# Two more raw weight buffers in the MLP, with a place of its own for block B22, in a tile that otherwise holds a branch's output

## The chip, the core and the metric

The kernel runs on one core of a Trainium2 chip. PE is the matrix engine (PEld its weight loads), DVE the vector engine, ACT the scalar engine, POOL and SP issue transfers here (POOL also does a few small operations). The metric is device time in microseconds (us) of one execution; runs without a profile give the median, and one execution with a profile gives the trace that is read below.

## The reference, cut to what matters

The program is two layers of an encoder trunk on 256 tokens of width 2048, all in float32. Each layer has a token-mixing half (one wide projection, three branches A, B and C, gates, an output projection) and an MLP half. The change lies in the MLP half:

```
D_MODEL, SEQ, DEPTH = 2048, 256, 2
D_FF = 4 * D_MODEL
for l in range(DEPTH):
    ...                                  # branches A, B, C, gates, merge
    x = x + merged @ w_out[l]
    h2 = rms_norm(x, norm2_g[l])
    u = jax.nn.relu(h2 @ w_up[l])        # (256, 2048) @ (2048, 8192)
    x = x + (u * u) @ w_down[l]          # (256, 8192) @ (8192, 2048)
return rms_norm(x, final_g)
```

## The kernel before, in words

**Weights.** 256 tokens make every product one pass over its weights, which come from HBM in pieces of 256 rows by 512 columns (512 KB, called a raw piece). Each piece is split into two parts that PE takes at its fast float32 rate: `whi`, a rounded copy made by ACT (L189, L207), and `wlo`, the rest, made by DVE (L190, L210). A product is three matmuls of 128x128 by 128x512 (L225, L226, L227): high by high, high by low, low by high.

**Slots.** The work is one list, `slots`, in the order in which PE runs it (`run_steps`). A plain slot is one raw piece: 12 matmuls. `ahead(i)`, called in the middle of slot i, writes the conversion of slot i+3 (`AHEAD = 3`, four pairs of `whi`/`wlo`), then `fetch`, which issues loads of further raw pieces on SP's queue, then `fetch_sums`. There are four raw buffers (`RAW_BUFS = 4`), and `st["free"]` counts how many pieces have been used up. SP issues its loads in the order of the program, and each waits until its buffer has been read, most often until DVE has written the `wlo` that reads it.

**The MLP.** Four times per layer, an up stage (four blocks of 512 columns of `w_up`, L243 and L244) makes a quarter of U = relu(h2 w_up)^2, and a down stage multiplies it by 2048 rows of `w_down`. The down stage goes over two column blocks at once (a pair, `add_pair`). A pair has eight steps s of 256 rows. Five of them are two plain slots each. The three steps in `SEVEN = (1, 3, 4)` take seven block products in place of eight: four slots `a`, `b`, `c`, `d` of 6, 6, 6 and 3 matmuls (`seven`). The 256 by 1024 piece of weights is cut into blocks B11, B12 (upper) and B21, B22 (lower). Slot `a` converts B11 and B21 (one raw piece); slots `b` and `c` convert four sums of blocks, held in a tile T called `tsum`; slot `d` converts B22. In the last quarter only the first pair is done so, and the other two blocks are plain units.

**T.** T has two places, taken in turn. A T is filled by a load on SP's queue (L182: B11 and B12), then by an adding transfer on POOL's queue, which waits for that load to land (L183: adds B12 and B22), and then by two additions on DVE in slot `a` (L208, L209). `fetch_sums` starts the T of the block after next once slot `c` has been written (`st["used"]`). So the T for s = 4 is started at slot `c` of s = 1, in the same pair.

**B22.** Before, B22 comes in a raw buffer of its own, of which it fills half (L168, 256 KB). Slot `a` takes both the buffer of B11/B21 and that of B22, and both count as free only after slot `d`.

**The tile.** The pool `yT` has two buffers, of 12 KB a partition, for the outputs of the branches (`ycT`, `yaT`, `ybT`) in turn. In the MLP one of them holds `SU`, the sums of U's blocks for the seven products; the other holds `ybT`, which is no longer read there.

Of the kernel before, what the change touches and what calls it, by code (L numbers as in the profile page):

```python
# [10 lines left out]
F32 = mybir.dt.float32  # L11
FR = mybir.dt.float32r
# [7 lines left out]
DEPTH = 2  # L20
# [11 lines left out]
BLK = 512  # L32
# [6 lines left out]
RAW_BUFS = 4  # L39
SEVEN = (1, 3, 4)  # L40
# [31 lines left out]
def encoder_trunk(ctx: ExitStack, tc: tile.TileContext, I, out: bass.AP):  # L72
    nc = tc.nc

    def pool(name, bufs=1, space=None):
        kw = {} if space is None else {"space": space}
        return ctx.enter_context(tc.tile_pool(name=name, bufs=bufs, **kw))

    one = pool("one")
    raw_p = pool("raw", RAW_BUFS)  # L80
    hl_p = pool("hl", AHEAD + 1)
    y_p = pool("yT", 2)
# [30 lines left out]
    def start(gen):  # L113
        lanes.append([gen, 0])
# [18 lines left out]


    slots, raws, summed = [], [], []
    st = {"dma": 0, "cv": 0, "free": 0, "sum": 0, "used": 0}
    raw_t, hl_t = {}, {}

    def add_raw(w, r, c, half=False):
        raws.append((w[r:r + 256, c:c + BLK], half))  # L140
        return len(raws) - 1

    def add_unit(w, r0, c0, nkc, act, after, form=None):
        u = {"act": act, "after": after, "n": nkc, "form": form}
        for s in range(nkc // 2):
            slots.append({"u": u, "s": s, "kind": "plain", "raw": add_raw(w, r0 + 256 * s, c0)})

    def add_pair(w, r0, c0, nkc, act, sums, half, middle, after):

        u = {"act": act, "after": after, "n": nkc, "form": "pair", "sums": sums, "half": half, "middle": middle}  # L150
        for s in range(nkc // 2):
            r = [add_raw(w, r0 + 256 * s, c0 + n * BLK, half=s in SEVEN and n == 1) for n in range(2)]
            if s in SEVEN:
                q = {"r": r, "w": w[r0 + 256 * s:r0 + 256 * (s + 1), c0:c0 + 2 * BLK], "i": len(summed)}
                summed.append(q)
                for kind in "abcd":
                    slots.append({"u": u, "s": s, "kind": kind, "q": q})
            else:
                for n in range(2):
                    slots.append({"u": u, "s": s, "kind": "plain", "raw": r[n], "n": n})  # L160

    def fetch(upto):
        while st["dma"] <= min(upto, len(raws) - 1):
            j = st["dma"]
            t = raw_p.tile([128, 2, BLK], F32, tag="raw", name="raw")
            src, half = raws[j]
            if half:
                nc.sync.dma_start(out=t[:, 1, :], in_=src[128:256, :])  # L168
            else:
                nc.sync.dma_start(out=t, in_=src.rearrange("(k p) f -> p k f", p=128))  # L170
            raw_t[j] = t
            st["dma"] += 1

    def fetch_sums():

        while L.get("T") is not None and st["sum"] < min(st["used"] + 2, len(summed)):
            q = summed[st["sum"]]
            if q["i"] >= L["T_end"]:
                return
            T = q["T"] = L["T"][:, q["i"] % 2]  # L180
            w = q["w"]
            nc.sync.dma_start(out=T[:, 1:3, :], in_=w[0:128, :].rearrange("p (n f) -> p n f", n=2))  # L182
            nc.gpsimd.dma_start(out=T[:, 1:3, :], in_=w[:, BLK:2 * BLK].rearrange("(k p) f -> p k f", p=128),  # L183
                                accum_op=ALU.add)
            st["sum"] += 1

    def lead(hi, lo, src):

        nc.scalar.activation(out=hi, in_=src, func=ACTF.Copy)  # L189
        nc.vector.tensor_tensor(out=lo, in0=src, in1=hi.bitcast(F32), op=ALU.subtract)  # L190

    def convert(upto):
        while st["cv"] <= min(upto, len(slots) - 1):
            sl = slots[st["cv"]]
            kind = sl["kind"]
            hi = hl_p.tile([128, 2, BLK], FR, tag="hi", name="whi")
            lo = hl_p.tile([128, 2, BLK], FR, tag="lo", name="wlo")
            if kind == "plain":
                lead(hi, lo, raw_t.pop(sl["raw"]))
                st["free"] += 1  # L200
            else:
                q = sl["q"]
                if kind == "a":
                    q["b0"], q["b1"] = [raw_t.pop(r) for r in q["r"]]
                b0, b1, T = q["b0"], q["b1"], q["T"]
                if kind == "a":
                    nc.scalar.activation(out=hi, in_=b0, func=ACTF.Copy)  # L207
                    nc.vector.tensor_tensor(out=T[:, 0, :], in0=T[:, 2, :], in1=b0[:, 0, :], op=ALU.add)  # L208
                    nc.vector.tensor_tensor(out=T[:, 3, :], in0=T[:, 0, :], in1=b0[:, 1, :], op=ALU.add)  # L209
                    nc.vector.tensor_tensor(out=lo, in0=b0, in1=hi.bitcast(F32), op=ALU.subtract)  # L210
                elif kind == "b":
                    lead(hi, lo, T[:, 0:2, :])
                elif kind == "c":
                    lead(hi, lo, T[:, 2:4, :])
                    st["used"] += 1
                else:
                    lead(hi[:, 1, :], lo[:, 1, :], b1[:, 1, :])
                    st["free"] += 2
            hl_t[st["cv"]] = (hi, lo)
            st["cv"] += 1  # L220

# [73 lines left out]

    def ahead(i):
        convert(min(i + AHEAD, 2 * i + 1))
        fetch(st["free"] - 1 + RAW_BUFS)
        fetch_sums()

    def four_banks(half, name):
# [122 lines left out]
    L = {}  # L424
# [323 lines left out]
    def after_up(n):  # L748
        def f(ps):
            c = L["c"]  # L750
            if n == 0:
                c["U"] = one.tile([128, KD, 2, S], FR, tag="Y", name="U")
                if "T" not in c:
                    c["T"] = True
                    L["T"] = one.tile([128, 2, 4, BLK], F32, tag="merged", name="tsum")
                    L["T_end"] = len(summed) * (c["l"] + 1) // DEPTH
            U = c["U"]
            E = [w2_p.tile([128, 2, S], F32, tag="E", name="u") for _ in range(2)]
            for tl, j0, w in L["groups"]:
                e = E[j0 // 2][:, j0 % 2:j0 % 2 + w, :]  # L760
                nc.scalar.activation(out=e, in_=tl[:, :, S:2 * S], func=ACTF.Copy)
                nc.vector.tensor_tensor(out=e, in0=tl[:, :, 0:S], in1=e, op=ALU.add)
            for e in E:
                nc.vector.scalar_tensor_tensor(out=e, in0=e, scalar=0.0, in1=e, op0=ALU.max, op1=ALU.mult)

            def task():
                for p in range(2):
                    k0 = 4 * n + 2 * p
                    split((U[:, k0:k0 + 2, 0, :], U[:, k0:k0 + 2, 1, :]), E[p])
                    if k0 // 2 in SEVEN:  # L770
                        if k0 // 2 == SEVEN[0]:
                            c["SU"] = y_p.tile([128, len(SEVEN), 2, 4, 128], FR, tag="yT", name="SU")
                        block_sums(c["SU"][:, SEVEN.index(k0 // 2)], E[p])
                    yield
            start(task())
        return f
# [190 lines left out]
    def then(f, g):  # L967
        def both(ps):
            f(ps)

            def later():
                yield
                yield
                yield
                g()
            start(later())
        return both

    for l in range(DEPTH):
        h_in = lambda: L["c"]["norm"].T  # L980
        w_in = I["w_in"][l]
        for unit in range(9):
            f = after_qkv(unit)
# [3 lines left out]
        for br, b, kcs, wname, yname in (("C", 2, 4, "w_proj_c", "ycT"), ("A", 0, 6, "w_proj_a", "yaT"),  # L987
                                         ("B", 1, 6, "w_proj_b", "ybT")):
            for n in range(NB):
                f = after_proj(br, n)  # L990
                if br == "C" and n == NB - 1:
                    f = then(f, queue_attention("B"))
# [15 lines left out]
    with tc.manual_schedule():  # L1008
        vin1 = w2_p.tile([16 * DEPTH, 128], F32, tag="yst", name="vin1")
        nc.sync.dma_start(out=ident, in_=I["c_ident"])  # L1010
        nc.scalar.dma_start(out=vin1, in_=I["norm1_g"].rearrange("l (k p) -> (l k) p", p=128))
        xin = I["x"][0].rearrange("(t p) d -> p t d", p=128)
        for b in range(NB):
            nc.sync.dma_start(out=x[:, :, b * BLK:(b + 1) * BLK], in_=xin[:, :, b * BLK:(b + 1) * BLK])
            fetch(b)
        nc.vector.memset(mhalf, -0.5)
        warm = sm_p.tile([128, 2], F32, tag="ms", name="warm")
        nc.scalar.activation(out=warm, in_=mhalf, func=ACTF.Copy)
        setup_norm1()
        L["c"] = new_layer(0)  # L1020
        norm = L["c"]["norm"]
        pieces = norm.transpose(0)
        next(pieces)
        convert(0)
        next(pieces)
        start(first_norm(norm))
        start(setup_all())
        run_steps()
# [33 lines left out]
```

## Time and profile before

| what | value |
|---|---|
| median of 3 runs without a profile | 2909.21 us (2907.08 to 2910.88) |
| the execution with the profile | 2915.21 us, of which the span is 2913.4 us |
| PE busy | 2862.0 us, 98% of the span |
| DVE, ACT busy | 1794.7 us (62%), 1425.3 us (49%) |
| mean granted clock of PE | 0.994 of full |
| read from HBM | 568.54 MB, 196 GB/s over the span |

A busy share of 98% doesn't say that PE runs at its own pace 98% of the time: the ends of matmuls are modelled, neighbours overlap, and a matmul at a lower clock counts as busy too. The starts of matmuls tell more.

### The profile page before, as it was taken

Reading aid. Unit: us, or ns where it says so; the run is one execution under the profiler, and the core shown is the slowest. Engines: PE = TensorE matmul, PEld = TensorE weight load, DVE = VectorE, ACT = ScalarE, POOL = GpSimd, SP = SyncE. Lnnn points to the kernel's source line nnn. Section 1 sums busy time; section 2 is a strip of 40 time slices with the busy share of each in tenths; the row PEclk is TensorE's granted clock in tenths of the full one; section 3 lists DMA queues with packets and bytes.
Section 4 is the critical chain, followed back from the end, with each engine's and each line's share of the span. In section 5 each row is a group of like instructions: output and inputs, shape, how many; then the busy total and the mean of one; then the engine's idle time right before and its main releaser. Section 6 shows DMA issues by size and latency. Waiting matters only on the chain.

```text
span 2913.4 us, 36216 instructions
## 1 busy us (share of the span) xinstructions
PE 2862.0 (98%) x13816; PEld 2371.6 (81%) x13816; DVE 1794.7 (62%) x2241; ACT 1425.3 (49%) x1818; POOL 155.5 (5%) x146
## 2 busy tenths in 40 slices
PE   9999999999999999999999999999999999999998
PEld 7888888888887878888788888888888878787886
DVE  5465454555677776776644654455556767767675
ACT  5455455444454544545544554454445445444454
POOL 1000001110000000000000000011000000000001
PEclk9999999999999999999999999999999999999999
DMA  7656665555767586675565565655556775856755
GB/s 234 200 151 191 196 175 170 193 183 187 215 205 224 184 243 195 210 219 183 188 214 186 153 197 189 187 161 190 188 187 203 219 229 184 247 179 217 232 180 181
DMA packets 287903, 573.06 MB, mean 197 GB/s; under 512 B 18196, under 2 KB 18382, under 8 KB 287600
## 3 DMA queue, kind: packets, MB, share of 16 engines
q1 hardware_dynamic: 272016, 534.64, 55.8%
q0 software_dynamic: 15376, 35.30, 7.7%
q8 instruction: 108, 1.77, 0.2%
q10 hardware_dynamic: 336, 0.80, 0.1%
q14 instruction: 67, 0.55, 0.1%
HBM read 568.54 MB, written 2.13 MB: 196 GB/s over the span
## 4 chain that ended last, share of the span: by engine, by line
PE 81%; DMA 9%; DVE 6%; issue 2%; ACT 2%; SPq 0%; POOLq 0%; ACTq 0%; DVEq 0%; POOL 0%
PE acc L225 17%; PE acc L226 17%; PE acc L227 17%; PE acc L243 16%; PE acc L244 8%; DMA raw<-in_w_down_dram 5%; DMA tsum<-in_w_down_dram 4%; DVE wlo L190 3%; ACT whi L189 1%; PE ob L553 1%; DVE wlo L210 1%; PE scb L521 0%; DVE tsum L208 0%; DVE x L819 0%; PE xt L400 0%
## 5 line engine op out<-in xcount | busy, mean ns | idle before, releaser
L190 DVE TENSOR_TENSOR wlo<-raw,whi 128x1024 fp32r<-128x1024 f32 (+1 forms) x950 | 1146.2, 1214 | 847.3 <-ACT whi L189 842.7
L189 ACT ACTIVATE whi<-raw 128x1024 fp32r<-128x1024 f32 (+1 forms) x950 | 980.1, 1038 | 928.1 <-PE acc L227 498.2
L243 PE MATMUL acc<-H,whi 128*128 128x512 f32 x2048 | 723.1, 398 | 0.0
L244 PE MATMUL acc<-H,wlo 128*128 128x256 f32 x2048 | 574.6, 281 | 0.0
L225 PE MATMUL acc<-whi,H 128*128 128x512 f32 x1408 | 564.8, 401 | 0.0
L227 PE MATMUL acc<-whi,H 128*128 128x512 f32 x1408 | 550.0, 391 | 0.0
L226 PE MATMUL acc<-wlo,H 128*128 128x512 f32 x1408 | 549.3, 390 | 0.4 <-DVE wlo L190 0.4
L243 PEld LDWEIGHTS acc<-H,whi 128*128 128x128 f32 x2048 | 384.7, 188 | 95.2 <-DVE x L722 0.6
L244 PEld LDWEIGHTS acc<-H,wlo 128*128 128x128 f32 x2048 | 386.7, 189 | 0.4
L225 PE MATMUL acc<-whi,U 128*128 128x512 f32 x772 | 307.0, 398 | 18.9 <-ACT whi L189 15.0
L226 PE MATMUL acc<-wlo,U 128*128 128x512 f32 x772 | 307.2, 398 | 9.6 <-DVE wlo L190 9.3
L225 PEld LDWEIGHTS acc<-whi,H 128*128 128x128 f32 x1408 | 264.9, 188 | 58.8 <-issue 8.1
L227 PEld LDWEIGHTS acc<-whi,H 128*128 128x128 f32 x1408 | 264.6, 188 | 56.8
L226 PEld LDWEIGHTS acc<-wlo,H 128*128 128x128 f32 x1408 | 265.2, 188 | 52.6 <-DVE wlo L190 1.2
L227 PE MATMUL acc<-whi,U 128*128 128x512 f32 x772 | 304.6, 395 | 0.0
L225 PEld LDWEIGHTS acc<-whi,U 128*128 128x128 f32 x772 | 147.2, 191 | 55.5 <-ACT whi L189 20.0
L226 PEld LDWEIGHTS acc<-wlo,U 128*128 128x128 f32 x772 | 147.4, 191 | 45.4 <-DVE wlo L190 15.4
L227 PEld LDWEIGHTS acc<-whi,U 128*128 128x128 f32 x772 | 147.7, 191 | 30.9
L183 POOL DMA_DIRECT2D tsum<-in_w_down_dram x42 | 50.7, 1220 | 1238.5 <-DMA tsum<-in_w_down_dram 1110.1
L189 ACT ACTIVATE whi<-tsum 128x1024 fp32r<-128x1024 f32 x84 | 87.1, 1053 | 33.3 <-DVE tsum L208 19.2
L225 PE MATMUL acc<-whi,M 128*128 128x512 f32 x256 | 101.2, 395 | 0.0
L190 DVE TENSOR_TENSOR wlo<-tsum,whi 128x1024 fp32r<-128x1024 f32 x84 | 99.6, 1219 | 2.1 <-ACT whi L189 2.1
(187 smaller groups left out, 2562.5 us busy)
## 6 DMA issues: line engine op xcount, KB each, us to landing
raw<-in_w_in_dram SPq DMA_DIRECT2D x352, 512.0 KB, 4.2
raw<-in_w_up_dram SPq DMA_DIRECT2D x256, 512.0 KB, 4.3
raw<-in_w_down_dram SPq DMA_DIRECT2D x214, 512.0 KB, 5.3
raw<-in_w_out_dram SPq DMA_DIRECT2D x64, 512.0 KB, 4.1
tsum<-in_w_down_dram SPq DMA_DIRECT2D x42, 512.0 KB, 4.5
tsum<-in_w_down_dram POOLq DMA_DIRECT2D x42, 512.0 KB, 8.0
raw<-in_w_proj_a_dram SPq DMA_DIRECT2D x24, 512.0 KB, 4.6
raw<-in_w_proj_b_dram SPq DMA_DIRECT2D x24, 512.0 KB, 3.5
```

The costliest lines, as they stand in the source:

```text
L183: nc.gpsimd.dma_start(out=T[:, 1:3, :], in_=w[:, BLK:2 * BLK].rearrange("(k p) f -> p k f", p=128), accum_op=ALU.add)
L189: nc.scalar.activation(out=hi, in_=src, func=ACTF.Copy)
L190: nc.vector.tensor_tensor(out=lo, in0=src, in1=hi.bitcast(F32), op=ALU.subtract)
L210: nc.vector.tensor_tensor(out=lo, in0=b0, in1=hi.bitcast(F32), op=ALU.subtract)
L225: nc.tensor.matmul(o, a[0], hi[:, kk, :], start=first, stop=False)
L226: nc.tensor.matmul(o, a[0], lo[:, kk, :], start=False, stop=False)
L227: nc.tensor.matmul(o, a[1], hi[:, kk, :], start=False, stop=last)
L243: nc.tensor.matmul(ps[j], hi[:, kk, fs], a[:, kc, :, :], start=first, stop=False)
L244: nc.tensor.matmul(ps[j][:, S:2 * S], lo[:, kk, fs], a[:, kc, 0, :], start=False, stop=last)
L553: nc.tensor.matmul(o[:, g, :], eT[:, 2 * g + kc, :], c["vb"][:, kc, col:col + 64], start=kc == 0, stop=kc == 1)
```

## The change

The pool `yT` gets a third kind of tile in the MLP, `rawx` (12 KB a partition, `more_room`), in the buffer that held `ybT`. A third of it holds the two B22 blocks of the two T places; the other two thirds are two more raw buffers, used for pieces of `w_up` and of `w_down`'s pairs alone. The counter `st["free"]` becomes a list `free` of free buffers, where None stands for one of the four of the pool `raw`. A buffer goes back to the list as soon as its piece's conversion has been written; that of B11/B21 goes back at slot `a`, not after `d`. B22 is loaded with its T, by `fetch_sums`, and `st["used"]` moves from slot `c` to slot `d`. The `rawx` buffers are dropped from the list when the next piece is not one of the MLP's.

```
-    st = {"dma": 0, "cv": 0, "free": 0, "sum": 0, "used": 0}
+    st = {"dma": 0, "cv": 0, "sum": 0, "used": 0}
+    free = [None] * RAW_BUFS
...
-    def fetch(upto):
-        while st["dma"] <= min(upto, len(raws) - 1):
-            j = st["dma"]
-            t = raw_p.tile([128, 2, BLK], F32, tag="raw", name="raw")
-            src, half = raws[j]
-            if half:
-                nc.sync.dma_start(out=t[:, 1, :], in_=src[128:256, :])
-            else:
-                nc.sync.dma_start(out=t, in_=src.rearrange("(k p) f -> p k f", p=128))
-            raw_t[j] = t
+    def fetch():
+
+        while free and st["dma"] < len(raws):
+            src, mlp = raws[st["dma"]]
+            b = free.pop(0)
+            if b is not None and not mlp:
+                continue
+            t = raw_p.tile([128, 2, BLK], F32, tag="raw", name="raw") if b is None else b
+            nc.sync.dma_start(out=t, in_=src.rearrange("(k p) f -> p k f", p=128))
+            raw_t[st["dma"]] = (t, b)
             st["dma"] += 1
 
+    def take(j):
+        t, b = raw_t.pop(j)
+        return t, lambda: free.append(b)
+
+    def more_room(c):
+
+        T = one.tile([128, 2, 4, BLK], F32, tag="merged", name="tsum")
+        c["SU"] = y_p.tile([128, len(SEVEN), 2, 4, 128], FR, tag="yT", name="SU")
+        X = y_p.tile([128, 6, BLK], F32, tag="yT", name="rawx")
+        L["T"] = [(T[:, i], X[:, i, :]) for i in range(2)]
+        L["T_end"] = len(summed) * (c["l"] + 1) // DEPTH
+        free.extend([X[:, 2:4, :], X[:, 4:6, :]])
...
-            T = q["T"] = L["T"][:, q["i"] % 2]
+            T, q["b22"] = L["T"][q["i"] % 2]
+            q["T"] = T
             w = q["w"]
             nc.sync.dma_start(out=T[:, 1:3, :], in_=w[0:128, :].rearrange("p (n f) -> p n f", n=2))
             nc.gpsimd.dma_start(out=T[:, 1:3, :], in_=w[:, BLK:2 * BLK].rearrange("(k p) f -> p k f", p=128),
                                 accum_op=ALU.add)
+            nc.sync.dma_start(out=q["b22"], in_=w[128:256, BLK:2 * BLK])
             st["sum"] += 1
...
             if kind == "plain":
-                lead(hi, lo, raw_t.pop(sl["raw"]))
-                st["free"] += 1
+                r, done = take(sl["raw"])
+                lead(hi, lo, r)
+                done()
             else:
...
                 if kind == "a":
-                    q["b0"], q["b1"] = [raw_t.pop(r) for r in q["r"]]
-                b0, b1, T = q["b0"], q["b1"], q["T"]
-                if kind == "a":
+                    b0, done = take(q["r"])
                     nc.scalar.activation(out=hi, in_=b0, func=ACTF.Copy)
...
                     nc.vector.tensor_tensor(out=lo, in0=b0, in1=hi.bitcast(F32), op=ALU.subtract)
+                    done()
...
                 elif kind == "c":
                     lead(hi, lo, T[:, 2:4, :])
+                else:
+                    lead(hi[:, 1, :], lo[:, 1, :], q["b22"])
                     st["used"] += 1
-                else:
-                    lead(hi[:, 1, :], lo[:, 1, :], b1[:, 1, :])
-                    st["free"] += 2
```

The order of instructions on PE, ACT, DVE and POOL stays as it is, row for row, apart from which buffer a row names; only SP's queue changes. 136 loads of 512 KB, 76 of `w_up` and 60 of `w_down`, now go into `rawx`, and so do the 42 loads of B22.

SP's queue in the first pair of a down stage, from the load of the piece behind step s = 1 on. Before; `tsum` at row 285 is the T for s = 4, 128x512 rows are B22 of s = 3 and s = 4, and the last two T's are for the next pair:

```order
L170 DMA raw_6365<-in_w_down_dram 128x2x512
L170 DMA raw_6387<-in_w_down_dram 128x2x512
L182 DMA tsum_5818<-in_w_down_dram 128x1024
L170 DMA raw_6479<-in_w_down_dram 128x2x512
L168 DMA raw_6481<-in_w_down_dram 128x512
L170 DMA raw_6493<-in_w_down_dram 128x2x512
L168 DMA raw_6505<-in_w_down_dram 128x512
L182 DMA tsum_5818<-in_w_down_dram 128x1024
L170 DMA raw_6560<-in_w_down_dram 128x2x512
L170 DMA raw_6562<-in_w_down_dram 128x2x512
L182 DMA tsum_5818<-in_w_down_dram 128x1024
```

The same place with the change, from the same load on:

```order
L173 DMA raw_6320<-in_w_down_dram 128x2x512
L173 DMA raw_6342<-in_w_down_dram 128x2x512
L173 DMA raw_6364<-in_w_down_dram 128x2x512
L173 DMA rawx_5820<-in_w_down_dram 128x2x512 x2
L200 DMA tsum_5818<-in_w_down_dram 128x1024
L203 DMA rawx_5820<-in_w_down_dram 128x512
L173 DMA raw_6489<-in_w_down_dram 128x2x512
L173 DMA raw_6501<-in_w_down_dram 128x2x512
L173 DMA raw_6512<-in_w_down_dram 128x2x512
L200 DMA tsum_5818<-in_w_down_dram 128x1024
L203 DMA rawx_5820<-in_w_down_dram 128x512
L173 DMA raw_6571<-in_w_down_dram 128x2x512
```

Before, the first two plain pieces behind s = 4 (the two loads `raw_6560` and `raw_6562`) stand behind the T for the next pair's s = 1. With the change they are the `x2` row ahead of the T for s = 4, and five or six loads of weights stand between the step that PE is at and the piece being loaded.

SP's queue in the first up stage of a layer, where the MLP's tiles are taken. Before:

```order
L170 DMA raw_5807<-in_w_up_dram 128x2x512
L170 DMA raw_5844<-in_w_up_dram 128x2x512
L182 DMA tsum_5818<-in_w_down_dram 128x1024 x2
L170 DMA raw_5880<-in_w_up_dram 128x2x512
L170 DMA raw_5902<-in_w_up_dram 128x2x512
```

With the change:

```order
L173 DMA raw_5807<-in_w_up_dram 128x2x512
L173 DMA rawx_5820<-in_w_up_dram 128x2x512 x2
L173 DMA raw_5848<-in_w_up_dram 128x2x512
L200 DMA tsum_5818<-in_w_down_dram 128x1024
L203 DMA rawx_5820<-in_w_down_dram 128x512
L200 DMA tsum_5818<-in_w_down_dram 128x1024
L203 DMA rawx_5820<-in_w_down_dram 128x512
L173 DMA raw_5885<-in_w_up_dram 128x2x512
```

Here two raw loads and two B22 loads are issued at one moment beside the two T loads.

## Rows read from the trace of the kernel before

**Rows 1.** Busy time by stage: eight down stages, and one up stage (1100.20)

```profile
core 0: us, PE busy (x) PEld busy (x) DVE busy (x) ACT busy (x) POOL busy (x), PEclk, DMA share, GB/s
824.30:915.10 90.80, 85.83 (x369) 68.09 (x368) 67.84 (x78) 45.89 (x50) 7.19 (x6) 1.00 0.76 228
1005.50:1100.20 94.70, 88.00 (x369) 69.90 (x368) 71.33 (x82) 45.51 (x50) 7.22 (x6) 0.96 0.77 228
1100.20:1190.60 90.40, 90.40 (x513) 78.35 (x512) 58.83 (x73) 42.62 (x50) 0.00 (x0) 1.00 0.59 186
1190.60:1281.50 90.90, 87.51 (x369) 70.76 (x368) 70.67 (x81) 46.08 (x50) 7.24 (x6) 0.96 0.80 235
1371.90:1465.30 93.40, 89.98 (x401) 73.80 (x400) 64.51 (x75) 49.31 (x67) 1.21 (x1) 0.98 0.57 186
2272.00:2363.20 91.20, 87.21 (x368) 69.26 (x367) 71.02 (x81) 45.54 (x50) 7.18 (x6) 0.98 0.78 234
2453.70:2544.80 91.10, 86.03 (x368) 69.59 (x367) 69.76 (x80) 45.90 (x50) 7.22 (x6) 0.98 0.78 231
2635.20:2726.10 90.90, 86.17 (x368) 69.50 (x367) 69.83 (x80) 45.72 (x50) 7.25 (x6) 0.98 0.77 233
2816.60:2904.30 87.70, 84.96 (x376) 70.06 (x375) 58.44 (x65) 43.18 (x55) 9.96 (x9) 1.00 0.53 177
```

**Rows 2.** Order of time on PE: first and last of 46 matmuls in a row

```profile
1199.73 0.39 PE L226 MATMUL acc<-wlo,U 128*128 128x512 f32 x1
...
1209.93 0.39 PE L226 MATMUL acc<-wlo,U 128*128 128x512 f32 x1
```

**Rows 3.** Who waited for whom: us in total, times, longest us

```profile
ACT whi L189 <- DMA raw<-in_w_down_dram: 132.3, 65, 8.0
...
PE acc L225 <- ACT whi L189: 15.0, 11, 3.0
...
DVE tsum L208 <- DMA tsum<-in_w_down_dram: 10.8, 12, 3.3
...
PE acc L226 <- DVE wlo L190: 9.7, 14, 0.8
...
PE psum L226 <- DVE wlo L210: 5.3, 7, 2.3
...
PE acc L225 <- ACT junk L410: 3.8, 2, 2.7
```

**Rows 4.** Chain that ended last in a down stage: start, us, what

```profile
1011.77 3.33 DMA tsum<-in_w_down_dram
...
1015.67 8.14 DMA tsum<-in_w_down_dram
...
1029.89 8.63 DMA raw<-in_w_down_dram
...
1075.26 9.40 DMA raw<-in_w_down_dram
...
1087.93 0.43 PE acc L227
...
1091.35 0.43 PE acc L226
```

**Rows 5.** Stretches of 5 us in that stage, same columns as Rows 1

```profile
1005.00:1010.00 5.00, 5.00 (x24) 4.16 (x23) 4.55 (x9) 3.57 (x6) 0.00 (x0) 1.00 0.05 14
1030.00:1035.00 5.00, 5.00 (x24) 4.14 (x23) 1.59 (x2) 0.34 (x1) 0.34 (x1) 1.00 1.02 285
1055.00:1060.00 5.00, 4.48 (x20) 3.33 (x20) 5.00 (x7) 2.76 (x3) 0.00 (x0) 1.00 0.14 46
1085.00:1090.00 5.00, 3.66 (x8) 2.57 (x9) 3.92 (x4) 3.33 (x4) 0.00 (x0) 0.52 1.06 267
```

**Rows 6.** Tile tsum: landing of SP's loads, then of POOL's adding transfers

```profile
DMA to landing us min/median/max: 3.3/4.5/7.1
...
DMA to landing us min/median/max: 5.8/8.0/14.7
```

More of the change, by code (lines that the diff above doesn't have):

```diff
@@ L135, in encoder_trunk, with add_raw @@
     slots, raws, summed = [], [], []
-    st = {"dma": 0, "cv": 0, "free": 0, "sum": 0, "used": 0}
+    st = {"dma": 0, "cv": 0, "sum": 0, "used": 0}
     raw_t, hl_t = {}, {}
-    def add_raw(w, r, c, half=False):
-        raws.append((w[r:r + 256, c:c + BLK], half))
+    free = [None] * RAW_BUFS
+    def add_raw(w, r, c, mlp=False):
+        raws.append((w[r:r + 256, c:c + BLK], mlp))
         return len(raws) - 1
@@ L145, in add_unit @@
         for s in range(nkc // 2):
-            slots.append({"u": u, "s": s, "kind": "plain", "raw": add_raw(w, r0 + 256 * s, c0)})
+            slots.append({"u": u, "s": s, "kind": "plain", "raw": add_raw(w, r0 + 256 * s, c0, form == "feature")})
     def add_pair(w, r0, c0, nkc, act, sums, half, middle, after):
@@ L151, in add_pair @@
         for s in range(nkc // 2):
-            r = [add_raw(w, r0 + 256 * s, c0 + n * BLK, half=s in SEVEN and n == 1) for n in range(2)]
             if s in SEVEN:
-                q = {"r": r, "w": w[r0 + 256 * s:r0 + 256 * (s + 1), c0:c0 + 2 * BLK], "i": len(summed)}
+                q = {"r": add_raw(w, r0 + 256 * s, c0, True), "w": w[r0 + 256 * s:r0 + 256 * (s + 1), c0:c0 + 2 * BLK],
+                     "i": len(summed)}
                 summed.append(q)
@@ L159, in add_pair @@
                 for n in range(2):
-                    slots.append({"u": u, "s": s, "kind": "plain", "raw": r[n], "n": n})
-    def fetch(upto):
-        while st["dma"] <= min(upto, len(raws) - 1):
-            j = st["dma"]
-            t = raw_p.tile([128, 2, BLK], F32, tag="raw", name="raw")
-            src, half = raws[j]
-            if half:
-                nc.sync.dma_start(out=t[:, 1, :], in_=src[128:256, :])
-            else:
-                nc.sync.dma_start(out=t, in_=src.rearrange("(k p) f -> p k f", p=128))
-            raw_t[j] = t
-            st["dma"] += 1
+                    slots.append({"u": u, "s": s, "kind": "plain", "n": n,
+                                  "raw": add_raw(w, r0 + 256 * s, c0 + n * BLK, True)})
+    def fetch():
[7 more added lines that the diff above has]
+            raw_t[st["dma"]] = (t, b)
+            st["dma"] += 1
+    def take(j):
[8 more added lines that the diff above has]
+        free.extend([X[:, 2:4, :], X[:, 4:6, :]])
     def fetch_sums():
@@ L198, in convert @@
             if kind == "plain":
-                lead(hi, lo, raw_t.pop(sl["raw"]))
-                st["free"] += 1
+                r, done = take(sl["raw"])
+                lead(hi, lo, r)
+                done()
             else:
                 q = sl["q"]
+                T = q["T"]
                 if kind == "a":
-                    q["b0"], q["b1"] = [raw_t.pop(r) for r in q["r"]]
-                b0, b1, T = q["b0"], q["b1"], q["T"]
-                if kind == "a":
+                    b0, done = take(q["r"])
                     nc.scalar.activation(out=hi, in_=b0, func=ACTF.Copy)
@@ L297, in ahead @@
         convert(min(i + AHEAD, 2 * i + 1))
-        fetch(st["free"] - 1 + RAW_BUFS)
+        fetch()
         fetch_sums()
@@ L752, in f @@
                 c["U"] = one.tile([128, KD, 2, S], FR, tag="Y", name="U")
[L753 to L756, printed above, removed]
+                if "SU" not in c:
+                    more_room(c)
             U = c["U"]
@@ L770, in task @@
                     if k0 // 2 in SEVEN:
-                        if k0 // 2 == SEVEN[0]:
-                            c["SU"] = y_p.tile([128, len(SEVEN), 2, 4, 128], FR, tag="yT", name="SU")
                         block_sums(c["SU"][:, SEVEN.index(k0 // 2)], E[p])
@@ L1014, in encoder_trunk @@
             nc.sync.dma_start(out=x[:, :, b * BLK:(b + 1) * BLK], in_=xin[:, :, b * BLK:(b + 1) * BLK])
-            fetch(b)
+            if b == 0:
+                room, free[1:] = free[1:], []
+            fetch()
+            free.extend(room[:1])
+            room = room[1:]
         nc.vector.memset(mhalf, -0.5)
```

## The prediction

> **What bounds the kernel now.** I read the page first. PE is busy for 98% of the span, so the question is whether the missing time has one place. The busy times by stage say where to look: the up stage shows 90.40 us of PE in 90.40 us, while every down stage shows 3 to 7 us of idle PE [rows 1]. Busy time understates the loss, so I count starts. From 1199.73 to 1209.93 there are 46 matmuls, 45 steps in 10.20 us: 0.227 us each, undisturbed [rows 2]. A down stage of two pairs has, per pair, 5 steps of 24 matmuls and 3 of 21, that is 366 in all: 83.1 us at that pace. The six full down stages took 90.8, 94.7, 90.9, 91.2, 91.1 and 90.9 us [rows 1], so they lost 7.7, 11.6, 7.8, 8.1, 8.0 and 7.8: 51 us. The two stages of the last quarters have 375 such matmuls (85.1 us) and 24 small transposes; of 93.4 and 87.7 us about 8 are lost, transposes allowed for. Sum: 59 us. The rest of the kernel I take as fixed, since the change moves nothing there.
>
> Then the waits. PE waited 11 times for a `whi` (15.0 us) and 14 times for a `wlo` of L190 (9.7 us) [rows 3]. Behind them stands ACT, which waited 65 times and 132.3 us for raw pieces of `w_down`. PE's third wait, `psum` for L210 (7 times, 5.3 us), is mostly another matter: L210 stands on DVE behind the additions into T, and DVE waited 12 times for T's transfers [rows 3]. The fourth, for `junk`, is the norm at the layer's end.
>
> Last, the chain in one down stage [rows 4]. It shows the two causes side by side. T's load for s = 4 takes 3.33 us and its adding transfer 8.14 us; both stand on the chain, so that T has no slack. Behind the next T a raw load of 1029.89 takes 8.63 us, and a later one 9.40 us. The reader is to see that these raw loads are slow because they are asked for late and all together: the transfer engines are 5% and 14% busy in two stretches of that stage (14 and 46 GB/s), and full (285 GB/s) in another [rows 5]. With four buffers, two of them held by a step in `SEVEN` from slot `a` to `d`, nothing can be fetched in the idle stretches.
>
> The clock adds to it. After the stall at 1085 the granted clock of that stretch is 0.52 [rows 5], the lower of its two levels (1.2 GHz), and from 1087.93 to 1091.35 nine matmuls in a row stand with 0.43 us each, not 0.227 [rows 4]. Nine times 0.20 is 1.8 us, and the step before them lost some too: 2 us.
>
> **The change, part by part.** *Work.* PE, ACT, DVE and POOL do the same instructions in the same order; no byte is added, since B22's 256 KB was a load of its own before too. This part costs nothing directly.
>
> *Two buffers more, and the early return of B11/B21's.* A raw piece is asked for when the one six pieces ahead is converted. A plain slot lasts 12 x 0.227 = 2.7 us, so six pieces last about 16 us of PE, four last 11, and before two of these four stood still for a step in `SEVEN`. The slowest raw loads in the chain take 8.6 and 9.4 us [rows 4], and these two come from the crowd behind a T. 16 us covers them; 11 less a held step of 4.8 (21 x 0.227) doesn't. So I take all waits of PE on raw pieces as gone: 15.0 + 9.7 us of idle time. Each of the 25 waits loses 0.16 us more than its idle time, as a matmul is shown with 0.39 us but steps by 0.227 [rows 2]: 4.1 us. Sum 28.8 us. Clock: six of the stages' rows stand below 1.00 [rows 1], the two at 0.96 with more than one stall each; I count six stretches of 1.4 to 2.0 us that follow raw stalls, 10 us. And of the seven `psum` waits I give the change one or two, where B11/B21 was late: 1.3 us. Total gain 40 us. Its bounds: nothing, if the loads still come late; and 59 less the 4.1 us of the `junk` waits, 55 us, if T's waits go too.
>
> *Bandwidth.* What hides the extra prefetch is idle transfer time. A stage moves 228 GB/s x 90.8 us = 20.7 MB [rows 1]; in 83.1 us that is 249 GB/s, below the 285 of a full stretch [rows 5]. If that cover were missing, the stage would be as long as its transfers: 20.7 MB at 285 GB/s is 73 us, still under PE's 83.
>
> *B22 and T.* B22's load now stands behind T's on SP and waits for slot `d`'s `wlo`. Behind it in SP's order stand raw loads that wait for later conversions anyway, so nobody is held. T's load itself stands where it stood: behind loads that wait for slot `a`, and waiting for slot `c`'s `wlo`. The new thing is what may be in flight before it. In the order, the last two raw loads ahead of T (into `rawx`) are released at `a` of s = 1 and before, while T waits for `c`; in the chain T's load went out at 1011.77 and took 3.33 us, the shortest of all its 42 [rows 4, 6], so the queue was empty. With the change I expect at most one landing load, at a price between 0 and 3.8 us (7.1 - 3.3 [rows 6]), nearer to 0, because the piece asked for at `a` has two slots to land. The adding transfer meets two or three raw loads as before; there I take 0, between -2.2 us (5.8, the shortest, against the median of 8.0 [rows 6]) and +1.4 us (9.4, as the slowest crowded raw load of the chain [rows 4]); the longest, 14.7, I leave to the place where two T's go out at once, the first up stage.
>
> The page "DMA: Bandwidth & Descriptors" of the Trainium skill (Issuing engines are not separate DMA queues) says that transfers from SP and POOL run on the same 16 engines and interleave. That speaks against the change: deeper prefetch on SP would stretch POOL's adding transfer, and by it the time would be the first rival's below, not the sum's. The range of 5.8 to 14.7 us in the trace agrees that something stretches it.
>
> *DVE.* It is busy 67.8 to 71.3 us in a full down stage [rows 1], 82 to 86% of 83.1 us, and at 1055 it is full for 5 us [rows 5]. That stretch is its catching up after late pieces; with pieces on time it has less to catch up. I leave 0 here.
>
> *First up stage of a layer.* Two raw, two T and two B22 loads at once: 2.6 MB with T's additions not counted, 9 us at 285 GB/s, against 16 us of pieces in hand. Hidden; if not, it is one wait per layer.
>
> *Sum.* 2915.2 - 40 = 2875 for an execution with a profile. That one stood 6.0 us above the median of the runs; taken off the median, 2909.2 - 40 = 2869. I predict the latter.
>
> **The rivals.**
>
> *T comes later.* There are 14 T's for s = 4, one for each pair (three quarters with two pairs and one with one, in two layers), and the one on the chain has no slack. If crowding adds 1.4 us to each adding transfer, 14 x 1.4 = 20 us come back: 2889. For: DVE's 12 waits for T [rows 3]. Against: the loads around T are about as many as before, and conversions that are on time start T earlier against PE.
>
> *T's waits go too.* If slot `c` of s = 1 is converted a microsecond earlier, the stalls on T (up to 5.3 us and one slow-clock stretch) shrink as well: gain about 50, 2859.
>
> *Loads late anyway.* The crowd behind two T's is 2 x 1.3 MB plus four raw pieces; if one in two of the stalls stays, the gain is 20: 2889.
>
> *Nothing.* SP issues in order. If the new loads stood behind a T load that waits, they would be early on paper alone: 2907. Against: the order puts the pieces behind s = 4 ahead of the T loads that they followed before.
>
> *Slower.* If T's load for s = 4 stands behind two raw loads in SP's queue in every pair, it takes 7.1 in place of 3.3 us [rows 6]: 14 x 3.8 = 53 us, and stalls that long bring a slow-clock stretch of 2 us each, 28 more. 2869 + 81 = 2950. It decides above (40 / 14) = 2.9 us per pair, less with the clock. Against: the queue was empty at that moment.
>
> **How the numbers follow.** Chances: forecast 0.60 (2862 to 2882), T later 0.15, T's waits gone too 0.10, loads late anyway 0.06, nothing 0.04, slower 0.05. The range takes in the forecast, both T rivals and the half gain: 2855 to 2897. Within 0.2% (5.8 us) a measurement of this kernel hardly tells a change. Faster by more: 0.60 + 0.15 + 0.10 + 0.06 less a little for their tails, 0.88; within 0.2%: 0.06; slower: 0.06.
>
> **What would show it.** Right: the full down stages at 84 to 86 us with a clock of 1.00; PE's waits for `whi` of L189 near 0 and ACT's for raw `w_down` pieces well below 132 us; stretches with idle transfer engines shorter; T's load for s = 4 still at 3.3 us. Wrong: raw waits gone but `psum` waits for L210 longer than 5.3 us, or SP's T loads with a median above 4.5 us, or new waits of PE in an up stage. The prediction fails if T, not raw, is what then ends last in each pair.

## The result, and the profile after

The kernel with the change takes 2874.95 us (median of 4 runs, 2873.28 to 2875.87); the kernel before took 2910.05 us beside it (4 runs, 2907.08 to 2913.95). The ratio is 0.9878, with a 95% interval of 0.9861 to 0.9895: some 35 us faster. The execution with the profile took 2875.01 us, its span 2873.2 us.

Line numbers moved with the change. L244 to L246 are the three matmuls of a product (L225 to L227 before), L208 and L209 `lead` (L189 and L190), L227 to L229 the additions into T and the `wlo` of slot `a` (L208 to L210), L200 and L201 T's load and its adding transfer (L182 and L183), L429 the norm (L410).

The busy times by stage, of the six full down stages and the two last quarters, with the columns of [rows 1]:

```profile
824.70:908.70 84.00, 83.37 (x368) 68.67 (x367) 72.19 (x82) 46.13 (x50) 7.18 (x6) 1.00 0.82 250
999.10:1084.10 85.00, 83.33 (x368) 68.67 (x367) 72.18 (x82) 46.11 (x50) 7.22 (x6) 1.00 0.82 249
1174.50:1259.00 84.50, 83.31 (x368) 68.68 (x367) 72.15 (x82) 46.12 (x50) 7.24 (x6) 1.00 0.82 252
1349.50:1442.40 92.90, 89.98 (x402) 73.71 (x400) 64.43 (x75) 49.36 (x67) 1.21 (x1) 0.98 0.51 167
2250.90:2335.60 84.70, 83.35 (x368) 68.67 (x367) 72.17 (x82) 46.13 (x50) 7.18 (x6) 1.00 0.82 249
2426.10:2511.40 85.30, 83.57 (x368) 68.55 (x368) 71.91 (x82) 45.92 (x50) 7.22 (x6) 1.00 0.81 246
2601.80:2686.10 84.30, 83.28 (x368) 68.62 (x367) 72.11 (x82) 46.07 (x50) 7.26 (x6) 1.00 0.83 252
2776.50:2864.10 87.60, 85.42 (x376) 70.08 (x375) 58.84 (x65) 43.14 (x55) 9.95 (x9) 1.00 0.46 156
```

Against 83.1 us at PE's undisturbed pace, the six full stages now lose 0.9, 1.9, 1.4, 1.6, 2.2 and 1.2 us: 9 us, where they lost 51. The gain lies there: the two last quarters stand as they stood but for 0.6 us, and the span outside the down stages is 2.2 us longer. The clock is at 1.00 in all six, where it was at 0.96 or 0.98 in five of them, and the transfers of a stage, at 246 to 252 GB/s, are what the same bytes in less time make.

The waits, us in total, times, longest:

```profile
DVE tsum L227 <- DMA tsum<-in_w_down_dram: 18.8, 9, 2.7
...
PE psum L245 <- DVE wlo L229: 10.5, 9, 1.8
...
PE acc L244 <- ACT junk L429: 2.2, 2, 1.1
```

Read this beside [rows 3]. No row is left in which ACT, DVE or PE waits for a raw piece of `w_down` (ACT's 132.3 us), and none in which PE waits for a `whi` of L208 (15.0 us). What grew is T: DVE's wait for it from 10.8 to 18.8 us, and PE's `psum` wait behind it from 5.3 to 10.5 us. Taken pair by pair, it grew in one place and shrank in another. Before, PE waited once in the eight first pairs of a down stage (2.3 us) and six times in the second pairs (3.0 us); with the change it waits in each of the eight first pairs (10.0 us) and once in a second pair (0.5 us).

The chain of one stage, which answers to [rows 4], shows T alone, with a longer adding transfer:

```profile
1005.42 3.16 DMA tsum<-in_w_down_dram
...
1009.14 9.86 DMA tsum<-in_w_down_dram
1019.02 0.70 DVE tsum L227
...
1021.63 0.50 PE psum L245
```

T's 42 loads on SP, then its 42 adding transfers on POOL, as in [rows 6]:

```profile
DMA to landing us min/median/max: 3.1/5.6/8.3
...
DMA to landing us min/median/max: 7.6/9.5/12.8
```

The shortest adding transfer of all now takes 7.6 us, where it took 5.8. The loads of the T's for s = 4 still take 3.1 to 4.4 us; the longer ones belong to the other 28 T's, for which DVE doesn't wait.

### The profile page after: what moved, and what is told of

Same layout as the page of the kernel before. It is cut to its first block, busy times and chain, and to the rows that moved or that the text cites. A ratio compares the mean times of both kernels' runs of the same rounds, so it can differ in the third digit from the quotient of the medians.

```text
span 2873.2 us, 36216 instructions
## 1 busy us (share of the span) xinstructions
PE 2844.0 (99%) x13816; PEld 2367.1 (82%) x13816; DVE 1799.6 (63%) x2241; ACT 1427.5 (50%) x1818; POOL 155.3 (5%) x146
## 4 chain that ended last, share of the span: by engine, by line
PE 92%; DMA 4%; DVE 2%; ACT 1%; issue 1%; SPq 0%; POOLq 0%; POOL 0%; DVEq 0%
PE acc L244 20%; PE acc L246 20%; PE acc L245 20%; PE acc L262 17%; PE acc L263 8%; DMA tsum<-in_w_down_dram 4%; PE psum L245 1%; PE psum L246 1%; DVE wlo L209 1%; PE psum L244 1%; PE ob L572 1%; PE scb L540 0%; PE xt L419 0%; PE sca L598 0%; ACT whi L208 0%
## 5 line engine op out<-in xcount | busy, mean ns | idle before, releaser
L209 DVE TENSOR_TENSOR wlo<-raw,whi 128x1024 fp32r<-128x1024 f32 x786 | 971.2, 1241 | 707.6 <-ACT whi L208 702.1
L208 ACT ACTIVATE whi<-raw 128x1024 fp32r<-128x1024 f32 x786 | 826.9, 1057 | 727.1 <-PE acc L246 504.7
L244 PE MATMUL acc<-whi,H 128*128 128x512 f32 x1408 | 564.9, 401 | 0.0
L246 PE MATMUL acc<-whi,H 128*128 128x512 f32 x1408 | 550.2, 391 | 0.0
L244 PEld LDWEIGHTS acc<-whi,H 128*128 128x128 f32 x1408 | 265.1, 188 | 58.8 <-issue 8.1
L246 PEld LDWEIGHTS acc<-whi,H 128*128 128x128 f32 x1408 | 264.7, 188 | 56.9
L244 PE MATMUL acc<-whi,U 128*128 128x512 f32 x772 | 301.5, 391 | 2.2 <-ACT junk L429 2.2
L245 PE MATMUL acc<-wlo,U 128*128 128x512 f32 x772 | 300.7, 390 | 0.0
L246 PE MATMUL acc<-whi,U 128*128 128x512 f32 x772 | 300.7, 390 | 0.0
L209 DVE TENSOR_TENSOR wlo<-rawx,whi 128x1024 fp32r<-128x1024 f32 (+1 forms) x164 | 177.2, 1086 | 99.2 <-ACT whi L208 96.7
L208 ACT ACTIVATE whi<-rawx 128x1024 fp32r<-128x1024 f32 (+1 forms) x164 | 155.1, 947 | 155.7 <-PE acc L246 79.6
L244 PEld LDWEIGHTS acc<-whi,U 128*128 128x128 f32 x772 | 144.9, 188 | 33.1 <-ACT junk L429 3.0
L246 PEld LDWEIGHTS acc<-whi,U 128*128 128x128 f32 x772 | 145.0, 188 | 30.4
L208 ACT ACTIVATE whi<-tsum 128x1024 fp32r<-128x1024 f32 x84 | 87.9, 1056 | 59.8 <-DVE tsum L227 25.0
L201 POOL DMA_DIRECT2D tsum<-in_w_down_dram x42 | 50.6, 1206 | 1198.0 <-DMA tsum<-in_w_down_dram 820.0
```

The source lines that it names most:

```text
L244: nc.tensor.matmul(o, a[0], hi[:, kk, :], start=first, stop=False)
L245: nc.tensor.matmul(o, a[0], lo[:, kk, :], start=False, stop=False)
L246: nc.tensor.matmul(o, a[1], hi[:, kk, :], start=False, stop=last)
```

## The experiments

Ten kernels, each timed against the kernel before on the same chip (medians of before: 2909.3, 2911.3 and 2910.3 us in three groups). The line numbers of a view are those of its own kernel: in own_place and the runs named after it they are one less than with the change, in t_late three more, and in spread_before those of the kernel before.

| run | raw buffers in the MLP | what else | us | ratio to before (95%) |
|---|---|---|---|---|
| own_place | 4 | B22's own place, early return | 2904.65 | 0.9975 (0.9965 to 0.9986) |
| two_more | 6 | B22 in a raw buffer, return after `d` | 2875.39 | 0.9879 (0.9865 to 0.9894) |
| one_more | 5 | as the change | 2879.82 | 0.9899 (0.9886 to 0.9912) |
| the change | 6 | | 2874.95 | 0.9878 (0.9861 to 0.9895) |
| hold | 6 | raw loads held back during T | 2862.99 | 0.9839 (0.9826 to 0.9852) |
| own_place_hold | 4 | the same | 2880.01 | 0.9895 (0.988 to 0.991) |
| t_late | 6 | T for s = 4 later | 2975.26 | 1.0225 (1.0208 to 1.0242) |
| spread | 6 | s = 1, 3, 5 | 2861.39 | 0.9827 (0.9812 to 0.9842) |
| spread_before | 4, kernel before | s = 1, 3, 5 | 2893.46 | 0.9944 (0.9928 to 0.9961) |
| own_place_spread | 4 | s = 1, 3, 5 | 2864.12 | 0.984 (0.9821 to 0.986) |
| hold_spread | 6 | both | 2862.76 | 0.9836 (0.9814 to 0.9857) |

### One part alone: own_place, two_more, one_more

own_place leaves the change's code and takes the two buffers away:

```
-        free.extend([X[:, 2:4, :], X[:, 4:6, :]])
```

Expected: 

> B22 in its own place and B11/B21's buffer back at slot a, but four raw buffers as before. If the number of pieces in hand makes the loads late (my reading), four pieces are 11 us of PE against loads of 8 to 9 us plus their conversion, so about half of the gain stays: 2885 to 2895 us, and ACT's waits for raw pieces of w_down fall from 132 us to some 30 to 70. If the buffers held by a step in SEVEN were the whole cause, it stands within 2 us of the change, 2875, with those waits near 0.

Measured 2904.65 us, outside both. Its nine runs lie in two groups, 2897.62 to 2898.86 us (four) and 2904.65 to 2905.71 us (five); the trace is of one at 2898.82, so differences taken from the median can be some 6 us too large. Its waits show why the gain is small:

```profile
ACT whi L207 <- DMA raw<-in_w_down_dram: 73.2, 38, 5.9
...
DVE tsum L226 <- DMA tsum<-in_w_down_dram: 37.6, 14, 3.8
...
PE psum L244 <- DVE wlo L228: 24.7, 14, 2.9
```

ACT still waits for raw pieces, if half as long as before, but in the down stages no row is left in which PE waits for the `whi` or `wlo` of a plain slot: its stalls on raw pieces are gone there with four buffers (in the first up stages of the layers 2.5 us of such waits are left). They are replaced by stalls on T, now in each of the 14 pairs. The raw waits use up the conversions' lead over PE, and T's load starts by a conversion. In the second pair of one stage, the matmul that begins slot `a` of s = 1 and T's load stand like this (start, us, engine, line):

```profile
1053.07 0.47 PE L243 MATMUL psum<-whi,U 128*128 128x512 f32 x1
...
1056.54 0.34 SPq L199 DMA_DIRECT2D tsum<-in_w_down_dram  x1
```

and with the change, in the same pair:

```profile
1048.07 0.39 PE L244 MATMUL psum<-whi,U 128*128 128x512 f32 x1
...
1047.94 0.34 SPq L200 DMA_DIRECT2D tsum<-in_w_down_dram  x1
```

T's load goes out 3.47 us behind that matmul in the one and 0.13 us ahead of it in the other. Over the six second pairs of full stages the mean of this difference is 3.14 us for own_place, 1.87 us before and -0.12 us with the change.

one_more gives back one of the two buffers:

```
-        free.extend([X[:, 2:4, :], X[:, 4:6, :]])
+        free.append(X[:, 2:4, :])
```

Expected: 

> As the change, with one raw buffer more in place of two. My reading: five pieces are 13.6 us of PE, nearly enough: 2876 to 2882 us, ACT's waits for raw w_down pieces under 15 us. If each buffer gave the same, it would lie halfway between the run with four buffers and the change.

2879.82 us, in the range of my reading. ACT's waits are not: where I expected under 15 us, they are 33.1 us for `raw` and 10.8 us for `rawx`. They don't reach PE in the down stages; its waits there are for T (`psum`, 14.1 us, 12 times). By the medians the first of the two buffers is worth 2904.65 - 2879.82 = 24.8 us and the second 4.9, which is hardly clear of noise (the two intervals overlap).

two_more is the other half: both buffers, while B22 stays in a raw buffer of its own, and both buffers of a step come back after slot `d`.

```
                 elif kind == "c":
                     lead(hi, lo, T[:, 2:4, :])
+                    st["used"] += 1
                 else:
-                    lead(hi[:, 1, :], lo[:, 1, :], q["b22"])
-                    st["used"] += 1
+                    lead(hi[:, 1, :], lo[:, 1, :], q["b1"][:, 1, :])
+                    q["done0"]()
+                    q["done1"]()
```

Expected: 

> Two raw buffers more, but B22 in a raw buffer of its own as before, and both buffers of a step in SEVEN back only after slot d. Six buffers less the two held leave four, as many as the run with B22's own place has: 2880 to 2892 us if only the free ones count. If the number alone counts, 2875 us.

2875.39 us: the number alone counts. B22's own place and the early return add nothing measurable to it. Its raw waits are not all gone (ACT, 23.1 and 4.6 us for `raw`, 13.3 and 2.0 us for `rawx`), but PE's wait is for T here too (`psum`, 16.7 us).

### What stretches T's adding transfer: hold, own_place_hold

hold keeps raw loads back from slot `d` of s = 1 until T for the next pair has been issued, so that they stand behind that load in SP's queue:

```
-        while free and st["dma"] < len(raws):
+        while free and st["dma"] < len(raws) and not (L.get("T") and st["used"] % 3 == 1):
...
-        fetch()
         fetch_sums()
+        fetch()
```

Expected: 

> As the change, but raw loads are held back from slot d of s = 1 until the T load for the next pair has been issued, so that the adding transfer of the T for s = 4 meets B22's load alone. If raw loads stretch that transfer (9.5 us median with the change, 8.0 before), it falls to 8 us or less in the first pairs, PE's psum wait for wlo from 10.5 us to 4 or less, and the time to 2864 to 2870 us. If the transfer is slow for another reason, it stays at 9.5 and the time at 2875. If the held loads are then late, ACT waits for raw pieces of w_down again and the time is above 2878.

2862.99 us, 12 us below the change and better than I expected. In the pair whose chain was shown, T's adding transfer, issued at 1006.78, landed after

```profile
DMA to landing us min/median/max: 5.9/5.9/5.9
```

where it took 9.9 us with the change. It lies between 5.8 and 6.1 us in the 12 pairs of full stages. The T's of s = 1 and s = 3, most of which meet raw loads, take 9 to 12 us, and nothing waits for them. Two of the full stages:

```profile
823.40:906.40 83.00, 83.00 (x369) 68.71 (x368) 72.15 (x82) 46.14 (x50) 7.18 (x6) 1.00 0.82 247
996.80:1079.70 82.90, 82.90 (x368) 68.65 (x367) 72.17 (x82) 46.19 (x50) 7.22 (x6) 1.00 0.80 246
```

PE has no idle time left there, and no loss against 83.1 us. In the last quarters the edit does nothing (adding transfers of 9.9 and 10.0 us): no T for a next pair is issued there, so nothing in SP's queue makes the held loads wait. Here the order of the queue held a load back only where something ahead of it waited.

own_place_hold is the same without the two buffers. Expected: 

> Four raw buffers and B22's own place, with raw loads held back as in the run hold. If the adding transfer's crowd is the whole matter and the two buffers only shift it, this stands near hold, 2863 us. If the two buffers are what lets loads be held, T's adding transfer falls to about 6 us, PE's psum waits go, and raw pieces come late in their place: ACT's waits for raw w_down pieces above 100 us, time 2890 to 2915 us.

2880.01 us, between my two cases: neither near 2863 nor above 2890.

```profile
ACT whi L207 <- DMA raw<-in_w_down_dram: 106.9, 80, 3.3
...
PE psum L244 <- DVE wlo L208: 3.0, 6, 0.5
...
PE psum L244 <- DVE wlo L228: 3.0, 2, 1.5
```

ACT waits for raw pieces as long as I expected, in 80 short waits (3.3 us at most), and they cost PE little. So an edit that takes no memory at all beyond B22's place, only the order of loads, is worth about 2904.65 - 2880.01 = 24.6 us, two thirds of the change's gain.

### The price of a late T: t_late

```
             if q["i"] >= L["T_end"]:
                 return
+            if q["i"] % 3 == 2 and not q.get("held"):
+                q["held"] = True
+                return
```

Expected: 

> As the change, but the load of the T for s = 4 goes out one slot later, behind a raw load that waits for the next conversion, some 3.7 us later. The price of a late T: in the 8 first pairs all of it is stall (they stall by 1.4 us now), in the 6 second pairs about 2.7 of it, so 8 x 3.7 + 6 x 2.7 = 46 us, and 10 to 25 us of slow clock behind 14 long stalls: 2930 to 2946 us, raw waits still 0. If T had slack that I don't see, 2875 to 2890.

2975.26 us, 100 us above the change, more than I expected. PE's wait and one stage:

```profile
PE psum L248 <- DVE wlo L232: 81.1, 14, 7.3
...
1014.10:1113.60 99.50, 87.53 (x368) 71.47 (x367) 72.18 (x82) 45.99 (x50) 7.22 (x6) 0.93 0.72 216
```

81.1 us in 14 waits is 5.8 us each, and 70.6 us more than with the change. The other 30 us are the cut in overlap (0.16 us a wait) and the clock, at 0.93 in that stage; how they divide wasn't measured. T's load goes out 3.6 us later against PE in the first pairs and 4.5 us later in the second, and beside the raw load ahead of it takes 5.0 to 5.5 us in place of 3.1 to 4.4. So in the full stages T lands about 5 us later in the first pairs and about 7 in the second, more than the 3.7 us that I had read off the order. Raw waits stay at 0. The price of a late T, which the rival *Slower* names, is here 100 / 14 = 7.2 us per pair.

### More time for T: spread, spread_before, own_place_spread, hold_spread

spread moves the third seven-product step one step later, from s = 4 to s = 5, and puts the six pieces of `middle_down` into four, since only four plain slots are left behind it:

```
-SEVEN = (1, 3, 4)
+SEVEN = (1, 3, 5)
```

Expected: 

> As the change, with the seven-product steps at s = 1, 3 and 5 in place of 1, 3 and 4, and the six pieces of work on their partial sums put into four slots. T for the last step then has a plain step more, 5.4 us. If late T's are all that is left in the down stages, PE's psum waits (10.5 us) and the slow clock after them go: 2860 to 2866 us. If the denser work on DVE at a pair's end holds PE, new waits stand at the pairs' starts: 2870 us or more.

2861.39 us. T's adding transfers are as slow as with the change (7.7 us at least, 9.2 in the middle), and no row of PE waiting for `psum` is left: PE's only wait in the MLP is for the norm (`acc L244 <- ACT junk L429: 3.7, 2, 1.9`). So slack for T does the same as a quick T. One stage of it:

```profile
997.70:1080.70 83.00, 83.00 (x369) 68.71 (x368) 70.96 (x81) 46.47 (x50) 7.22 (x6) 1.00 0.84 250
```

spread_before makes the same edit in the kernel before. Expected: 

> The kernel before with the steps at s = 1, 3 and 5. If the crowd of two T's close together made the raw loads late, most of the gain comes without any buffer: 2870 to 2880 us. If four buffers with two held are too few whatever the crowd, 2890 to 2908 us, with ACT's raw w_down waits still above 60 us.

2893.46 us, the second case: ACT waited 70.8 us (L189) and 99.0 us (L207) for raw pieces. Without the change, with buffers held from `a` to `d`, slack for T takes 18 us off.

own_place_spread has four raw buffers, B22's own place and s = 1, 3, 5. Expected: 

> Four raw buffers, B22's own place, and the steps at s = 1, 3, 5. In the run own_place no stall of PE ended in a raw load; its loss was late T's (24.7 us of psum waits for L228's wlo) and DVE's catching up. If early return plus slack for T is enough, 2861 to 2868 us, within 0.3% of spread, and the two buffers buy nothing beside it. If the two buffers are needed, raw waits come back: 2875 to 2890 us.

2864.12 us: the first case. ACT's raw waits are 21.2 and 1.6 us; in the down stages PE's wait for the norm stands alone (3.9 us), and 0.6 us of waits are left in up stages. The two buffers buy nothing that can be measured beside the slack for T. But B22's own place and the early return do: this run is 2893.46 - 2864.12 = 29.3 us below spread_before, from which it differs by them alone.

hold_spread has both edits. Expected: 

> The change with both edits: raw loads held back and the steps at s = 1, 3, 5. Either alone leaves no loss in the full down stages, so together nothing more is to be had there: 2859 to 2863 us, the same as spread within 0.1%. If the held loads come late after a step at s = 5, ACT's raw waits return and the time is 2865 us or more.

2862.76 us, the same as either alone, within what the measurement tells. Five of its six runs lie between 2860.42 and 2863.00 us; the sixth took 8494.02 us, for a reason that isn't known, and the ratio leaves it out. At 82.9 to 83.0 us in the stages shown above, against 83.1 undisturbed, the full down stages have nothing more to give.

## Why the prediction was right, and where its steps were not

**The sum.** Forecast 2869, range 2855 to 2897; measured 2874.95. On the profile's own scale the sum was 2915.2 - 40 = 2875, and the profiled execution took 2875.01. The step that failed is the last: taking the 40 off the median. It held the 6.0 us between the profiled execution and the median of before for a fixed part. With the change that distance is 0.06 us (2875.01 against 2874.95). A likely reading, not shown, is that stalls differ from run to run: the profiled execution stands 5.8 us below the median in own_place and 5.3 above it in two_more, which stall, and within 0.6 us of it in the four kernels that stall little (hold, spread, own_place_spread, hold_spread). By that reading a gain read off stalls belongs to the execution that shows them.

That the 40 came out to the microsecond is luck. The `psum` term was forecast as 1.3 us fewer and came as 5.2 us more, and the rest of the span, taken as fixed, is 2.2 us longer: 8.7 us to the bad. The stages made up for it. The clock's 10 us are borne out: matmuls that step by 0.4 us or more without a wait cost 12.2 us in the eight down stages before, and 1.6 with the change. Waits that the sum left out went too (1.6 us of `junk`, 1.0 us of `psum` for a `wlo` of L190). And what a stall costs beside its idle time, put at 4.1 us for 25 of them, must have been some 5 us more; that is what is left over, not a measurement.

**Raw pieces.** "I take all waits of PE on raw pieces as gone": right, the 15.0 and 9.7 us are 0. The stages came out at 84.0 to 85.3 us with a clock of 1.00, where 84 to 86 was forecast, and SP's load of the T for s = 4 stayed short (3.16 us in the chain shown).

**Why the buffers matter.** "16 us covers them; 11 less a held step of 4.8 doesn't." Only partly right. With four buffers, the early return and B22's own place, PE doesn't stall on a raw piece in a down stage either (own_place), but the time stays at 2904.65. What the prediction missed is that raw pieces and T are coupled: late raw pieces eat up the lead of the conversions, a conversion starts T's load, and raw loads slow T's adding transfer. Give T slack (own_place_spread, 2864.12) and four buffers are enough; give it none, and two more buffers pay by letting T start earlier in the second pairs (1.87 us to -0.12 us against PE).

**B22's own place and the early return.** Costed together with the two buffers. Apart, they are worth 5 us by the medians and 7 by the ratio, and nothing beside two more buffers (2874.95 against 2875.39); once T has slack they are worth 29 us and the buffers nothing. Either half is enough for the raw pieces; what it brings depends on T.

**T's adding transfer.** Taken as 0, between -2.2 and +1.4 us: mis-sized. The median rose by 1.5 us, just above the upper bound. The first rival, *T comes later*, was right in its mechanism: in the chain shown the adding transfer takes 9.9 us with raw loads beside it, and in the same place 5.9 us without them (hold). With that agrees what the Trainium skill says in "DMA: Bandwidth & Descriptors" (Issuing engines are not separate DMA queues), that transfers from SP and POOL share engines and interleave. It came to 5.2 us of `psum` waits, not to 20, because the second rival, *T's waits go too*, held at the same time: in the first pairs, where T's load goes out no earlier than before (0.8 us behind PE in both), the longer transfer costs 7.7 us more; in the second pairs, where the load goes out 2 us earlier, 2.5 us of waits went. They did not cancel to the forecast's 0.

Two of the prediction's own signs of being wrong came, therefore: `psum` waits longer than 5.3 us, and a median of SP's T loads above 4.5 us (5.6). T, not raw, is now what ends last in nine of the fourteen pairs, which it named as the way to fail. It held even so because these waits are short, 1.8 us at most, against the 24.7 us of raw waits that went.

**DVE, bandwidth, first up stage.** Costed at 0: right. DVE is busy 71.9 to 72.2 us a stage (67.8 to 71.3 before), still below PE's 83.1; the stages move 246 to 252 GB/s, and no row has PE waiting in an up stage.

**Slower.** T's load met an empty queue, as argued, so the rival's trigger didn't come. Its price holds up: 53 us of waits were put at 81 us with the clock, 1.5 times as much; in t_late the waits grew by 70.6 us and the time by 100, 1.4 times. What was too low, in what I expected of t_late, is how late a T becomes that is asked for 3.7 us later.

## What to carry to other kernels

When several streams feed one engine, find the one with no slack before adding buffers to the one with the longest waits: the longest waits here were for raw pieces, while giving the tight stream quiet (hold) or time (spread) was worth some 25 and 41 us in the kernel with four buffers (own_place), where two more buffers were worth 30, and 12 to 14 us on top of those. Undo each half of a change by itself, and again once the tight stream has slack: here B22's place and the early return were worth nothing beside the two buffers, but 29 us with slack for T, where the buffers were worth nothing. And count a loss by the starts of matmuls against their undisturbed step; the busy share was 98% with 59 us lost.

## What the hardware showed that I had not expected

T's 512 KB adding transfer takes 5.8 to 6.1 us when next to nothing moves beside it (in the pair of hold that was shown, B22's 256 KB landed 0.6 us after the transfer was issued), and in the chain shown 9.9 us beside three raw loads, the load of the next T and its B22. Two of those raw loads, issued at 9.88 and 12.34 us after 1000, were slow too and landed after

```profile
DMA to landing us min/median/max: 8.3/8.3/8.3
...
DMA to landing us min/median/max: 7.5/7.5/7.5
```

against medians of 4.7 us (`raw`) and 5.2 us (`rawx`) for loads of `w_down`. They stand beside one another as well, so how much of this the adding transfer does is not shown. From 1010 to 1015 the transfer engines were 85% busy and moved 224 GB/s, in the next 5 us they were full and moved 323, while a full stretch before moved 285 [rows 5]:

```profile
1010.00:1015.00 5.00, 5.00 (x23) 4.14 (x23) 4.62 (x5) 2.12 (x2) 0.34 (x1) 1.00 0.85 224
1015.00:1020.00 5.00, 4.96 (x22) 3.76 (x21) 1.64 (x3) 1.81 (x3) 0.00 (x0) 1.00 1.01 323
```

So GB/s alone doesn't say when the engines are full: bytes differ in what they cost. From the issue of that adding transfer to its landing (1009.14 to 1019.00), SP's queue and POOL's took, in packets, MB and share of the engines' time:

```profile
q1 hardware_dynamic: 927, 1.98, 59.0%
q0 software_dynamic: 272, 0.52, 29.8%
```

A byte of the adding transfer held the engines 1.9 times as long as a byte of the loads beside it (29.8 / 0.52 against 59.0 / 1.98). Together the two kept the engines 89% busy. That this is what stretched both is a reading; no run here tests it.
